# One 512-column matmul for the tokens' high and low halves in the stationary-weight projections

## The chip, the cores and the metric

The kernel runs on one core of a Trainium2 chip. The metric is the device time of one execution in microseconds; the time of the kernel before is the median of three runs.

## What is computed

Two transformer blocks run one after the other on 256 tokens of 2048 channels, in fp32. The first block has two attention layers (one of them with an indexer that selects keys) with a gated output. The second has sparse attention, a gated delta rule and a feed-forward part with 5632 inner channels. Cut to the products that matter here:

```
proj  = rms_norm(x) @ w_in                         # q, k, v, gates; second block: conv inputs, merge gates
o     = attention(q, k, v) * sigmoid-like gate     # the gate is a projection
x     = x + o @ w_out
mixed = g_nsa * (o_nsa @ w_up_nsa) + g_dn * (o_dn @ w_up_dn)
x     = x + mixed @ w_o
x     = x + (silu(h2 @ w_ffn_gate) * (h2 @ w_ffn_up)) @ w_ffn_down
```

## The kernel before, in words

Activations stay in SBUF and every weight is streamed once from DRAM. To keep fp32 accuracy each operand of a product is split into a high and a low part of type fp32r, and a product is three matmuls: high times high, high times low, low times high. The split activations are kept transposed, as pairs of tiles `hi` and `lo` of 128 channels x 4 chunks x 256 tokens (`new_T`, L206 to L209); a full input is four such pairs.

`gemm` (L117 to L160) multiplies the activations with 512 columns of a weight matrix. Its loop over `g` takes 512 rows of the weights at a time: one DMA of 1 MB on SP's queue into `raw` (L134, three buffers), then two tiles of weights, each of two chunks of 128 rows. For each tile ScalarE casts the high part `wh` (L139) and VectorE subtracts the low part `wl` (L140); both have three buffers. After each chunk's matmuls `tick` (L158) advances background work (attention heads, the delta rule), which is written as generators and interleaved with the products in this way. A framework planner then orders each engine's instructions when the program is built.

There are two forms of the product. In the plain one the tokens are stationary and 512 weight columns move (L155 to L157). In the flipped one (`flip=True`) the weights are stationary and 256 tokens move: for each of four blocks of 128 output columns there are three matmuls of 256 columns (L148 to L150), the first with the high tokens, the second with the low tokens, the third with the low weights:

```
o = pt[m // 2][:, (m % 2) * T:(m % 2 + 1) * T]
nc.tensor.matmul(o, wh[:, c, ms], hi[:, kc], start=first and m % 2 == 0, stop=False)
nc.tensor.matmul(o, wh[:, c, ms], lo[:, kc], start=False, stop=False)
nc.tensor.matmul(o, wl[:, c, ms], hi[:, kc], start=False, stop=last and m % 2 == 1)
```

The result of a flipped product is two PSUM banks, each with two blocks of 128 columns x 256 tokens. At the product's end `evac(b, psum)` is called for either bank. PSUM has four such banks (`mm`), taken one at a time.

The flipped form is used for the gate projection of both attention layers (L578, eight products), the inputs of the convolution (L1255, six), the two merge gates (L1276 and L1285, eight), the two up-projections of the mixers (L1278 and L1297, eight products of half the depth), and the feed-forward's gate and up projections (L1329 and L1338, 22). Their evacuations are one VectorE operation that reads PSUM and applies a per-token factor (L573, L1255, L1265, L1327, L1335) or combines it with a gate (L1278, L1290), followed by the nonlinearity and, where the result is the next product's input, by a new split (`split_into`, L521). The feed-forward part takes its inner channels in three blocks of four, four and three column blocks; each block does gate and up projections and then a plain product with `w_ffn_down`.

A helper `slot` (L51) gives temporary tiles out of the buffers of the split activations, alternately from `hi` and `lo` (eight buffers each).

Of the kernel before, what the change touches and what calls it, by code (L numbers as in the profile page):

```python
# [11 lines left out]
F32 = mybir.dt.float32  # L12
F32R = mybir.dt.float32r
# [4 lines left out]
P = 128  # L18
T = 256
# [7 lines left out]
class Kern:  # L27
    """The whole forward pass; activations stay in SBUF, weights stream through once."""

    def __init__(self, ctx, tc, d, out, stop=None):  # L30
# [9 lines left out]
        self.flip = False  # L40
        self.finished = set()

# [32 lines left out]
    def defer(self, n, fn):  # L75
        """trace fn after n further ticks"""
        self.later.append([n, fn])
# [14 lines left out]
    def tick(self):  # L92
        """advance deferred work and the background chains"""
# [27 lines left out]
    def gemm(self, xT, W, c0, n, evac, ng=4, split=False, flip=False):  # L121
# [3 lines left out]
        pt = [self.ps.tile([P, 512], F32, tag="mm", bufs=4, name="mm") for _ in range(2)]  # L125
        for g in range(ng):
# [8 lines left out]
            hi, lo = xT[g]  # L135
            for h in range(2):
                wh = self.sb.tile([P, 2, n], F32R, tag="wh", bufs=3, name="wh")
                wl = self.sb.tile([P, 2, n], F32R, tag="wl", bufs=3, name="wl")
                nc.scalar.copy(wh, raw[:, 2 * h:2 * h + 2])  # L139
                nc.vector.tensor_tensor(wl, raw[:, 2 * h:2 * h + 2], wh.bitcast(F32), ALU.subtract)  # L140
                for c in range(2):
# [9 lines left out]
                    for t in range(0 if flip else 2):  # L151
                        o = pt[t][:, :n]
# [6 lines left out]
        for t in range(2):  # L159
            evac(t, self.c2(pt[t]) if flip else pt[t][:, :n])  # L160
# [18 lines left out]
    def gemm_by_tile(self, xT, W, c0, n, evac, ng):  # L179
        """a narrow gemm that keeps its split weights and ends one token tile before the other"""  # L180
        nc = self.nc
        ws = []
        for g in range(ng):
# [3 lines left out]
            for h in range(2):  # L187
# [4 lines left out]
                ws.append((wh, wl))  # L192
        for t in range(2):
            o = self.ps.tile([P, 512], F32, tag="mm", bufs=4, name="mm")[:, :n]
            ts = slice(t * P, (t + 1) * P)
            for g in range(ng):
                hi, lo = xT[g]
# [8 lines left out]
    def new_T(self):  # L206
        hi = self.sb.tile([P, 4, T], F32R, tag="hi", bufs=8, name="hi")
        lo = self.sb.tile([P, 4, T], F32R, tag="lo", bufs=8, name="lo")
        return hi, lo  # L209

    def to_T(self, src, gain=None, scale=None):
        """src(t, c): [128 tokens, 128 channels]; returns the split transpose of 4 chunks."""
        nc = self.nc
        hi, lo = self.new_T()
# [21 lines left out]
        return hi, lo  # L236
# [7 lines left out]
    def rsq(self, out, in_, mul, n, eps=EPS):  # L244
        """out = (in_ * mul + eps) ** -0.5"""
# [8 lines left out]
    def norm_rstd(self, ss, dst=None):  # L254
        """ss: per token tile [128, 4] block sums of squares -> (rstd, rstd / 2, rstd^2 / 128)"""
# [11 lines left out]
    def rope4(self, o, x, tC, tS, scal=None, heads=4, hd=128):  # L267
        """o = x * C + swap(x) * S over [128, heads, hd]; x in PSUM or SBUF; scal per partition."""
# [20 lines left out]
    def trans4(self, src, dst, scale=None, n=4, eng=None):  # L289
        """dst [128, n*128] = per-128-column-chunk transposes of src [128, n*128]."""  # L290
# [36 lines left out]
    def park_x(self):  # L327
        """the residual waits in DRAM while the mixers need its room"""
# [22 lines left out]
    def gains2(self):  # L351
        """per-channel columns of the second block: conv taps, position embeddings, norm gain"""
# [1156 lines left out]
```

## Time and profile before

| what | value |
|---|---|
| median of 3 runs | 2310.97 us (2310.82 to 2311.34) |
| span of the profiled execution (its own time is not given beside it) | 2308.8 us |
| TensorE matmul, weight load | 2295.5 us, 2094.7 us busy |
| VectorE, ScalarE, GpSimd | 1395.8, 1089.4, 133.6 us busy |
| granted TensorE clock | 0.999 of full |
| moved by DMA | 404.70 MB, mean 175 GB/s |

A page of the profile names engines PE (TensorE matmuls), PEld (TensorE weight loads, which overlap matmuls), DVE (VectorE), ACT (ScalarE), POOL (GpSimd) and SP (SyncE). `L148` is line 148 of the kernel. Rows of grouped instructions have the line, engine, operation, output <- inputs by the program's names, shapes, count, then total busy time in us, mean in ns, and the idle time before them with what ended it. The ends of matmuls are modelled and consecutive records overlap, so the sum of their durations is longer than the time they take.

### The profile page before, as it was taken

Reading aid. Unit: us, or ns where it says so; the run is one execution under the profiler, and the core shown is the slowest. Engines: PE = TensorE matmul, PEld = TensorE weight load, DVE = VectorE, ACT = ScalarE, POOL = GpSimd, SP = SyncE. Lnnn points to the kernel's source line nnn. Section 1 sums busy time; section 2 is a strip of 40 time slices with the busy share of each in tenths; the row PEclk is TensorE's granted clock in tenths of the full one; section 3 lists DMA queues with packets and bytes.
Section 4 is the critical chain, followed back from the end, with each engine's and each line's share of the span. In section 5 each row is a group of like instructions: output and inputs, shape, how many; then the busy total and the mean of one; then the engine's idle time right before and its main releaser. Section 6 shows DMA issues by size and latency. Waiting matters only on the chain.

```text
span 2308.8 us, 39431 instructions
## 1 busy us (share of the span) xinstructions
PE 2295.5 (99%) x16446; PEld 2094.7 (91%) x16446; DVE 1395.8 (60%) x2073; ACT 1089.4 (47%) x1758; POOL 133.6 (6%) x233
## 2 busy tenths in 40 slices
PE   9999999999999999999999999999999999999998
PEld 8878998888998888999999999889998899989997
DVE  5686765656665656878675655555555455554555
ACT  5555644456544434564534444454443344433444
POOL 1011100112100300011101000000000000000000
PEclk9999999999999999999999999999999999999999
DMA  7544455654556754344443665555555555555554
GB/s 230 193 149 153 140 183 182 189 176 137 167 183 208 240 157 152 112 164 130 146 148 120 205 225 183 182 192 191 183 183 189 192 184 183 183 182 184 182 185 143
DMA packets 209811, 404.70 MB, mean 175 GB/s; under 512 B 7376, under 2 KB 25776, under 8 KB 209632
## 3 DMA queue, kind: packets, MB, share of 16 engines
q1 hardware_dynamic: 206880, 394.04, 52.5%
q0 software_dynamic: 2752, 8.13, 1.2%
q8 instruction: 129, 2.11, 0.4%
q14 instruction: 50, 0.41, 0.1%
HBM read 397.95 MB, written 4.19 MB: 174 GB/s over the span
## 4 chain that ended last, share of the span: by engine, by line
PE 99%; DMA 0%; DVE 0%; SPq 0%; ACT 0%; issue 0%; ACTq 0%; POOLq 0%; POOL 0%
PE mm L150 16%; PE mm L148 16%; PE mm L149 16%; PE mm L157 14%; PE mm L156 14%; PE mm L155 14%; PE lg L440 1%; PE tr L294 1%; PE tp L219 1%; PE hid L994 1%; PE nl L1086 0%; PE pt L473 0%; PE ib L638 0%; DMA x<-in_x_dram 0%; PE ov L490 0%; PE ov L491 0%
## 5 line engine op out<-in xcount | busy, mean ns | idle before, releaser
L140 DVE TENSOR_TENSOR wl<-raw,wh 128x1024 fp32r<-128x1024 f32 (+4 forms) x760 | 902.6, 1188 | 794.2 <-ACT wh L139 793.1
L139 ACT CAST wh<-raw 128x1024 fp32r<-128x1024 f32 (+4 forms) x760 | 775.9, 1021 | 1028.5 <-PE mm L149 550.3
L150 PE MATMUL mm<-hi,wl 128*128 128x256 f32 x3072 | 868.9, 284 | 0.0
L148 PE MATMUL mm<-hi,wh 128*128 128x256 f32 x3072 | 868.4, 283 | 0.0
L149 PE MATMUL mm<-lo,wh 128*128 128x256 f32 x3072 | 868.1, 283 | 0.0
L148 PEld LDWEIGHTS mm<-hi,wh 128*128 128x128 f32 x3072 | 579.8, 189 | 1.5 <-issue 0.5
L149 PEld LDWEIGHTS mm<-lo,wh 128*128 128x128 f32 x3072 | 579.2, 189 | 0.8 <-issue 0.2
L150 PEld LDWEIGHTS mm<-hi,wl 128*128 128x128 f32 x3072 | 577.9, 188 | 1.0 <-issue 0.2
L156 PE MATMUL mm<-wl,hi 128*128 128x512 f32 (+4 forms) x1504 | 574.6, 383 | 0.2 <-DVE wl L140 0.2
L157 PE MATMUL mm<-wh,lo 128*128 128x512 f32 (+4 forms) x1504 | 570.6, 381 | 0.0
L155 PE MATMUL mm<-wh,hi 128*128 128x512 f32 (+4 forms) x1504 | 529.3, 382 | 0.0
L156 PEld LDWEIGHTS mm<-wl,hi 128*128 128x128 f32 x1504 | 283.3, 188 | 55.4 <-issue 0.6
L157 PEld LDWEIGHTS mm<-wh,lo 128*128 128x128 f32 x1504 | 283.1, 188 | 55.0 <-issue 1.5
L155 PEld LDWEIGHTS mm<-wh,hi 128*128 128x128 f32 x1504 | 281.1, 189 | 56.2 <-issue 1.3
L248 POOL TENSOR_SCALAR rsqv<-nsum 128x1 f32<-128x1 f32 x10 | 3.5, 351 | 1228.4 <-DVE nsum L1361 744.4
L233 ACT ACTIVATE hi<-tp,gT 128x256 fp32r<-128x256 f32 x64 | 27.6, 471 | 21.3 <-PE tp L219 18.9
L454 ACT ACTIVATE lg<-lg,nb 128x128 f32<-128x128 f32 (+1 forms) x64 | 28.4, 445 | 16.7 <-POOL nb L447 16.7
L234 DVE SCALAR_TENSOR_TENSOR lo<-tp,gT,hi 128x256 fp32r<-128x256 f32 x64 | 28.4, 478 | 12.4 <-ACT hi L233 12.0
L730 DVE SCALAR_TENSOR_TENSOR cv<-raw,cols,cv 128x255 f32<-128x255 f32 (+2 forms) x72 | 31.1, 475 | 1.8 <-ACT cv L727 1.7
L252 ACT ACTIVATE junk<-x 128x512 bf16<-128x512 f32 (+1 forms) x42 | 25.6, 610 | 6.0 <-DMA x<-in_x_dram 2.2
L252 ACT ACTIVATE junk<-mm 128x128 bf16<-128x128 f32 x80 | 22.2, 278 | 7.3 <-PE mm L157 5.8
L440 PE MATMUL lg<-kT,qT 128*128 128x256 f32 (+1 forms) x128 | 23.7, 327 | 0.0
(378 smaller groups left out, 1386.2 us busy)
## 6 DMA issues: line engine op xcount, KB each, us to landing
raw<-in_w_in_dram SPq DMA_DIRECT2D x76, 1024.0 KB, 5.1
raw<-in_w_ffn_gate_dram SPq DMA_DIRECT2D x44, 1024.0 KB, 5.2
raw<-in_w_ffn_up_dram SPq DMA_DIRECT2D x44, 1024.0 KB, 5.2
raw<-in_w_ffn_down_dram SPq DMA_DIRECT2D x41, 1024.0 KB, 5.1
raw<-in_a_w_in_dram SPq DMA_DIRECT2D x40, 1024.0 KB, 5.1
raw<-in_b_w_in_dram SPq DMA_DIRECT2D x40, 1024.0 KB, 5.1
raw<-in_a_w_out_dram SPq DMA_DIRECT2D x16, 1024.0 KB, 5.0
raw<-in_b_w_out_dram SPq DMA_DIRECT2D x16, 1024.0 KB, 5.1
```

What stands on the lines that cost most here:

```text
L139: nc.scalar.copy(wh, raw[:, 2 * h:2 * h + 2])
L140: nc.vector.tensor_tensor(wl, raw[:, 2 * h:2 * h + 2], wh.bitcast(F32), ALU.subtract)
L148: nc.tensor.matmul(o, wh[:, c, ms], hi[:, kc], start=first and m % 2 == 0, stop=False)
L149: nc.tensor.matmul(o, wh[:, c, ms], lo[:, kc], start=False, stop=False)
L150: nc.tensor.matmul(o, wl[:, c, ms], hi[:, kc], start=False, stop=last and m % 2 == 1)
L155: nc.tensor.matmul(o, xh, wh[:, c], start=first, stop=False)
L156: nc.tensor.matmul(o, xh, wl[:, c], start=False, stop=False)
L157: nc.tensor.matmul(o, xl, wh[:, c], start=False, stop=last)
L234: nc.vector.scalar_tensor_tensor(lo[:, k], tp[:, c], g, hi[:, k].bitcast(F32), ALU.mult, ALU.subtract)
L252: self.nc.scalar.activation(self.junk()[:, :w], in_, AF.Square, accum_out=accum)
L440: nc.tensor.matmul(lb[:, i * S:(i + 1) * S], qT[:, h * P:(h + 1) * P], kT[:, :S], start=True, stop=True)
L730: v.scalar_tensor_tensor(o[:, s:], x[:, :T - s], self.convw[:, k:k + 1], o[:, s:], ALU.mult, ALU.add)
```

## The change

The high and low parts of the split activations lie in one tile `hl` of 128 x 4 chunks x 2 x 256, so that a chunk's high and low tokens are 512 adjacent columns. Flipped products become a function of their own, `gemm_T`. It does 256 output columns at a time (`b`), with two blocks of 128 columns, one PSUM bank each. A block takes one matmul of 512 columns (high weights; the results of the high and the low tokens land in two halves of the bank) and one of 256 columns (low weights on high tokens, added to the first half). The bank's halves are added at the evacuation (`joined`): ScalarE copies the second half, VectorE adds the first. A load is 1 MB as before, now 8 chunks of 256 columns. PSUM banks are taken in pairs. The plain product is left as it is but for the pair of banks, and so is the narrow product at the end.

```diff
+    def banks(self):
+        return self.ps.tile([P, 2, 512], F32, tag="mm", bufs=2, name="mm")
+
+    def weights(self, raw, h, n):
+        nc = self.nc
+        k = raw.shape[1] // 2
+        wh = self.sb.tile([P, k, n], F32R, tag="wh", bufs=3, name="wh")
+        wl = self.sb.tile([P, k, n], F32R, tag="wl", bufs=3, name="wl")
+        nc.scalar.copy(wh, raw[:, k * h:k * h + k])
+        nc.vector.tensor_tensor(wl, raw[:, k * h:k * h + k], wh.bitcast(F32), ALU.subtract)
+        return wh, wl
...
-                    for m in range(4 if flip else 0):
-                        o = pt[m // 2][:, (m % 2) * T:(m % 2 + 1) * T]
-                        ms = slice(m * P, (m + 1) * P)
-                        nc.tensor.matmul(o, wh[:, c, ms], hi[:, kc], start=first and m % 2 == 0, stop=False)
-                        nc.tensor.matmul(o, wh[:, c, ms], lo[:, kc], start=False, stop=False)
-                        nc.tensor.matmul(o, wl[:, c, ms], hi[:, kc], start=False, stop=last and m % 2 == 1)
...
+    def gemm_T(self, xT, W, c0, evac, ng=4):
+        nc = self.nc
+        for b in range(2):
+            pt = self.banks()
+            for g2 in range(ng // 2):
+                self.flush(lambda: len(xT) > 2 * g2 + 1 and None not in xT[2 * g2:2 * g2 + 2])
+                raw = self.sb.tile([P, 8, T], F32, tag="raw", bufs=3, name="raw")
+                nc.sync.dma_start(raw, W[g2 * 1024:(g2 + 1) * 1024,
+                                         c0 + b * T:c0 + (b + 1) * T].rearrange("(c p) n -> p c n", p=P))
+                for h in range(2):
+                    wh, wl = self.weights(raw, h, T)
+                    hl = xT[2 * g2 + h][2]
+                    for c in range(4):
+                        first = g2 == 0 and h == 0 and c == 0
+                        last = g2 == ng // 2 - 1 and h == 1 and c == 3
+                        for m in range(2):
+                            ms = slice(m * P, (m + 1) * P)
+                            nc.tensor.matmul(self.c2(pt[:, m]), wh[:, c, ms], hl[:, c],
+                                             start=first, stop=False)
+                            nc.tensor.matmul(pt[:, m, :T], wl[:, c, ms], hl[:, c, 0],
+                                             start=False, stop=last)
+                        if c % 2:
+                            self.tick()
+            p4 = pt.rearrange("p m (s n) -> p m s n", s=2)
+            evac(b, p4[:, :, 0], p4[:, :, 1])
...
+    def joined(self, o, p, q, row=None):
+        self.nc.scalar.copy(o, q)
+        self.nc.vector.tensor_tensor(o, p, o, ALU.add)
+        if row is not None:
+            self.nc.vector.tensor_tensor(o, o, row, ALU.mult)
...
     def new_T(self):
-        hi = self.sb.tile([P, 4, T], F32R, tag="hi", bufs=8, name="hi")
-        lo = self.sb.tile([P, 4, T], F32R, tag="lo", bufs=8, name="lo")
-        return hi, lo
+        hl = self.sb.tile([P, 4, 2, T], F32R, tag="hl", bufs=8, name="hl")
+        return hl[:, :, 0], hl[:, :, 1], hl
...
     def slot(self, name, dt=F32):
-        self.flip = not self.flip
-        return self.sb.tile([P, 2, 512], dt, tag="hi" if self.flip else "lo", bufs=8, name=name)
+        if self.half is not None:
+            b, self.half = self.half, None
+        else:
+            t = self.sb.tile([P, 2, 2, 512], F32, tag="hl", bufs=8, name="half")
+            b, self.half = t[:, 0], t[:, 1]
+        return b if dt is F32 else b.bitcast(dt)
```

Each evacuation of a flipped product takes the two halves and calls `joined` in the place of its first VectorE operation; the up-projections of the mixers join into a tile of their own before they are combined. In the feed-forward part, for example:

```diff
-                def evac_g(b, ps):
-                    v.tensor_tensor(s[b], ps, row, ALU.mult)
+                def evac_g(b, p, q):
+                    self.joined(s[b], p, q, row)
                     nc.scalar.activation(s[b], s[b], AF.Silu)
-                self.gemm(h2, d["w_ffn_gate_2"][0], 512 * jb, 512, evac_g, flip=True)
+                self.gemm_T(h2, d["w_ffn_gate_2"][0], 512 * jb, evac_g)
```

## Rows read from the trace of the kernel before

**Rows 1.** The page: busy time of each engine, and the chain that ended last.
```profile
PE 2295.5 (99%) x16446; PEld 2094.7 (91%) x16446; DVE 1395.8 (60%) x2073; ACT 1089.4 (47%) x1758; POOL 133.6 (6%) x233
...
PE 99%; DMA 0%; DVE 0%; SPq 0%; ACT 0%; issue 0%; ACTq 0%; POOLq 0%; POOL 0%
```

**Rows 2.** TensorE's waits, all execution: us in total, times, longest us.
```profile
PE warm L311 <- DVE zero L308: 1.7, 1, 1.7
...
PE mm L156 <- DVE wl L140: 0.2, 1, 0.2
```

**Rows 3.** Groups of TensorE instructions, shapes apart: busy us, mean ns, idle us.
```profile
L150 PE MATMUL mm<-hi,wl 128*128 128x256 f32 x3072 | 868.9, 284 | 0.0
L148 PE MATMUL mm<-hi,wh 128*128 128x256 f32 x3072 | 868.4, 283 | 0.0
```

**Rows 4.** Timeline of ScalarE, feed-forward part: start us, us, instruction [idle before].
```profile
1651.31 1.05 ACT L139 CAST wh<-raw 128x1024 fp32r<-128x1024 f32 x1 [1.80 <-PE mm L149]
...
1662.70 1.05 ACT L139 CAST wh<-raw 128x1024 fp32r<-128x1024 f32 x1 [1.79 <-PE mm L149]
...
1742.31 1.05 ACT L139 CAST wh<-raw 128x1024 fp32r<-128x1024 f32 x1 [1.73 <-PE mm L157]
...
1759.05 1.05 ACT L139 CAST wh<-raw 128x1024 fp32r<-128x1024 f32 x1 [1.74 <-PE mm L157]
...
1854.82 1.05 ACT L139 CAST wh<-raw 128x1024 fp32r<-128x1024 f32 x1 [1.83 <-PE mm L149]
...
1866.34 1.05 ACT L139 CAST wh<-raw 128x1024 fp32r<-128x1024 f32 x1 [1.83 <-PE mm L149]
...
2013.10 1.05 ACT L139 CAST wh<-raw 128x1024 fp32r<-128x1024 f32 x1 [1.70 <-PE mm L157]
...
2029.90 1.05 ACT L139 CAST wh<-raw 128x1024 fp32r<-128x1024 f32 x1 [1.75 <-PE mm L157]
```

**Rows 5.** Timeline of TensorE where 512 columns give way to 256.
```profile
2282.30 0.39 PE L157 MATMUL mm<-wh,lo 128*128 128x512 f32 x1
2282.53 0.40 PE L155 MATMUL mm<-wh,hi 128*128 128x256 f32 x2
2282.76 0.28 PE L156 MATMUL mm<-wl,hi 128*128 128x256 f32 x1
```

**Rows 6.** Groups of ScalarE and VectorE instructions that read 512 elements from PSUM.
```profile
L298 ACT COPY qT<-tr 128x512 f32<-128x512 f32 x20 | 11.6, 584 | 8.9 <-PE tr L294 8.6
...
L1327 DVE TENSOR_TENSOR sg<-mm,row 128x512 f32<-128x512 f32 x22 | 15.2, 691 | 0.3
```

**Rows 7.** Windows: PE, PEld, DVE, ACT, POOL busy us; PEclk; DMA share; GB/s.
```profile
1025.00:1050.00 25.00, 25.00 (x217) 25.00 (x216) 22.99 (x37) 13.76 (x22) 2.71 (x4) 1.00 0.51 166
...
1571.00:1594.00 23.00, 23.00 (x196) 23.00 (x195) 11.35 (x12) 10.72 (x11) 0.00 (x0) 1.00 0.55 184
1775.00:1797.00 22.00, 22.00 (x97) 17.83 (x96) 10.69 (x11) 8.39 (x8) 0.00 (x0) 1.00 0.57 191
```

**Rows 8.** Timeline of VectorE at the end of an up-projection.
```profile
1593.76 1.40 DVE L1335 TENSOR_TENSOR up<-mm,row 128x512 f32<-128x512 f32 x2
...
1596.28 1.22 DVE L140 TENSOR_TENSOR wl<-raw,wh 128x1024 fp32r<-128x1024 f32 x1
```

**Rows 9.** DMA of 1571 to 1640 us, then of 2271 to 2288 us.
```profile
q1 hardware_dynamic: 6336, 12.58, 55.9%
...
raw<-in_w_ffn_gate_dram SPq DMA_DIRECT2D x8, 1024.0 KB, 5.2
...
q1 hardware_dynamic: 1779, 1.77, 32.4%
...
raw<-in_w_ffn_down_dram SPq DMA_DIRECT2D x5, 512.0 KB, 3.4
```

**Rows 10.** Timeline at the start of the feed-forward part, TensorE and VectorE.
```profile
1547.37 0.28 PE L148 MATMUL mm<-hi,wh 128*128 128x256 f32 x1
...
1556.99 0.48 DVE L234 SCALAR_TENSOR_TENSOR lo<-tp,gT,hi 128x256 fp32r<-128x256 f32 x1
```

More of the change, by code (lines that the diff above doesn't have):

```diff
@@ L39, in __init__ @@
         self.later = []
-        self.flip = False
+        self.half = None
         self.finished = set()
@@ L118, in ready, with gemm @@
             yield
-    def gemm(self, xT, W, c0, n, evac, ng=4, split=False, flip=False):
+    def banks(self):
+        return self.ps.tile([P, 2, 512], F32, tag="mm", bufs=2, name="mm")
+    def weights(self, raw, h, n):
         nc = self.nc
-        pt = [self.ps.tile([P, 512], F32, tag="mm", bufs=4, name="mm") for _ in range(2)]
+        k = raw.shape[1] // 2
[4 more added lines that the diff above has]
+        return wh, wl
+    def gemm(self, xT, W, c0, n, evac, ng=4, split=False):
+        nc = self.nc
+        pt = self.banks()
         for g in range(ng):
@@ L134, in gemm @@
                 nc.sync.dma_start(raw, src)
-            hi, lo = xT[g]
+            hi, lo, _ = xT[g]
             for h in range(2):
[L137 to L140, printed above, removed]
+                wh, wl = self.weights(raw, h, n)
                 for c in range(2):
@@ L144, in gemm @@
                     last = g == ng - 1 and kc == 3
-                    for m in range(4 if flip else 0):
-                        o = pt[m // 2][:, (m % 2) * T:(m % 2 + 1) * T]
-                        ms = slice(m * P, (m + 1) * P)
-                        nc.tensor.matmul(o, wh[:, c, ms], hi[:, kc], start=first and m % 2 == 0, stop=False)
-                        nc.tensor.matmul(o, wh[:, c, ms], lo[:, kc], start=False, stop=False)
-                        nc.tensor.matmul(o, wl[:, c, ms], hi[:, kc], start=False, stop=last and m % 2 == 1)
-                    for t in range(0 if flip else 2):
-                        o = pt[t][:, :n]
+                    for t in range(2):
+                        o = pt[:, t, :n]
                         xh = hi[:, kc, t * P:(t + 1) * P]
@@ L159, in gemm @@
         for t in range(2):
-            evac(t, self.c2(pt[t]) if flip else pt[t][:, :n])
+            evac(t, pt[:, t, :n])
+    def gemm_T(self, xT, W, c0, evac, ng=4):
+        nc = self.nc
+        for b in range(2):
+            pt = self.banks()
+            for g2 in range(ng // 2):
[19 more added lines that the diff above has]
+            evac(b, p4[:, :, 0], p4[:, :, 1])
     @staticmethod
@@ L192, in gemm_by_tile @@
                 ws.append((wh, wl))
+        pt = self.banks()
         for t in range(2):
-            o = self.ps.tile([P, 512], F32, tag="mm", bufs=4, name="mm")[:, :n]
+            o = pt[:, t, :n]
             ts = slice(t * P, (t + 1) * P)
             for g in range(ng):
-                hi, lo = xT[g]
+                hi, lo, _ = xT[g]
                 for c in range(4):
@@ L572, in evac @@
                 gt, th = self.c2(self.w2("gt")), self.c2(self.w2("gth"))
-                nc.vector.tensor_tensor(gt, ps, row, ALU.mult)
+                self.joined(gt, p, q, row)
                 nc.scalar.activation(th, gt, AF.Tanh)
@@ L1148, in values @@
                 b = o[t].rearrange("p (h q) -> p h q", h=4)
-                hi, lo = (x[:, :, t * P:(t + 1) * P] for x in dst)
+                hi, lo = (x[:, :, t * P:(t + 1) * P] for x in dst[:2])
                 nc.scalar.copy(hi, b)
@@ L1253, in second @@
                 raw = [self.c2(self.ev(f"raw{b}")) for b in range(2)]
-                self.gemm(hT, W, 2584 + 1024 * i + 512 * g, 512,
-                          lambda b, ps: v.tensor_tensor(raw[b], ps, row, ALU.mult), flip=True)
+                self.gemm_T(hT, W, 2584 + 1024 * i + 512 * g,
+                            lambda b, p, q: self.joined(raw[b], p, q, row))
                 self.start((kind, g), self.dn_conv(kind, g, raw, st[g]), "de"[g])
@@ L1262, in second, with mgate @@
         md = []
-        def mgate(m, ps):
-            v.tensor_tensor(m, ps, rowh, ALU.mult)
+        def mgate(m, p, q):
+            self.joined(m, p, q, rowh)
             nc.scalar.activation(m, m, AF.Tanh)
```

42 lines of the change are left out of this document (23 added, 19 removed).

## The prediction

> **What bounds the kernel now.** I read the shares and the chain of waits first. TensorE is busy for 2295.5 of 2308.8 us, and the chain that ended last is TensorE for 99% of its length [rows 1]. The waits of TensorE say the same: there are four in the whole execution, the longest 1.7 us and the shortest 0.2 us [rows 2]. So time can only be won by taking time out of TensorE's stream, and only be lost by putting a wait into it.
>
> A busy TensorE is not yet a rate, because records overlap: the 256-column matmuls are shown with 284 ns each [rows 3], though 9216 of them at that length would be longer than the span. The true spacing comes from ScalarE's weight casts. Each cast waits for TensorE to release a tile, so cast after cast shows how long one tile of weights keeps TensorE. A tile is 24 matmuls of 256 columns in the stationary-weight products, and 12 of 512 columns in the others.
>
> - Stationary weights, first block of the feed-forward part: four intervals between 1651.31 and 1662.70, 2.848 us each [rows 4], so **118.7 ns** per matmul.
> - The same in the second block: four intervals between 1854.82 and 1866.34, 2.880 us each [rows 4], so **120.0 ns**. I see no reason in the rows for this 1%.
> - 512 columns: six intervals between 1742.31 and 1759.05, 2.790 us each [rows 4], so **232.5 ns**.
>
> Two matmuls of 256 columns thus cost 237.4 ns, one of 512 costs 232.5. What the change can win on TensorE is this difference, some 5 ns each time two become one.
>
> **What is removed on TensorE.** Today one block of 128x128 weights takes three matmuls of 256 columns: high weights on high tokens, high weights on low tokens, low weights on high tokens. Each line has 3072 [rows 3], and that is 48 products of 64 blocks. Afterwards a block takes one matmul of 512 and one of 256 columns, so 3072 matmuls and as many weight loads go.
>
> - Old tile: 2.848 us. New tile, 8 of each width: 8 x 232.5 + 8 x 118.7 = 2.809 us. Saved 0.039 us.
> - 14 of the 48 products (gate and up of the feed-forward's second and third blocks, seven column blocks) run at the slower pace: there 512 columns are at 2.800 us a tile too, six intervals between 2013.10 and 2029.90 [rows 4], or 233.3 ns. 2.880 us against 8 x 233.3 + 8 x 120.0 = 2.827 us. Saved 0.053 us.
> - 48 products have 8 tiles each. (34 x 8) x 0.039 + (14 x 8) x 0.053 = 10.6 + 5.9 = **16.5 us**.
>
> The new operand shape does not stand in the trace: widths that alternate matmul by matmul. The nearest row is where the stream changes from 512 to 256 columns: the last 512 keeps its 0.23 us and the first two of 256 take 0.23 us together [rows 5], so that step adds nothing. The step from 256 back to 512 is not shown. I bound the pair from both sides. Below: the small matmul at half the price of the large, 116.3 ns, which would save 25 us instead of 16.5. Above: no gain at all, the joint matmul at the price of two. I take the sum of the two measured spacings, since both widths, with a fresh weight load ahead of each matmul, are what those rows timed.
>
> The Trainium skill ("TensorE: Matmul & The Clock Gate", section "Back-to-back issue gap") gives an isolated gap of N/2.4 + 2.5 ns, so a dropped matmul would be worth 2.5 ns and the change, as an estimate, 3072 x 2.5 = 7.7 us. The trace does not agree with that page: its 118.7 and 232.5 ns are well above the page's 109.2 and 215.8, and my sum goes by the trace.
>
> **What is added beside it.** The evacuation of a half product has one ScalarE copy out of PSUM and one VectorE addition more. There are 52 products (eight have half the depth), so 104 halves. At 0.58 us for a copy of 512 elements and 0.69 us for a VectorE operation of the same size [rows 6], that is 60 us of ScalarE and 72 us of VectorE. Per half (about 11.2 us) 0.6 and 0.7 us go into engines which in the feed-forward stage are busy 10.7 and 11.35 of 23 us [rows 7]. I cost it at nothing: weight tiles are triple-buffered, so when a half ends two later tiles are ready and cover about 5.6 us.
>
> How that cover is used today can be seen at an up-projection's end. VectorE begins to evacuate at 1593.76 and the next low-half subtraction runs at 1596.28, 1.22 us long [rows 8]: it is done 3.7 us after the product ended, with 1.9 us to spare. Afterwards VectorE handles 512 elements instead of 1024 at a time, but waits for ScalarE's copy first: 0.58 + 3 x 0.69 + 1.22 = 3.9 us, or 4.9 us if a 1.05 us cast [rows 4] is placed ahead of the copy. Still within 5.6 us, but by 0.7 to 1.7 us. This is the thinnest part of my argument.
>
> **Edits that cost nothing, and why.**
>
> - Loads: four of 1 MB per full product before and after, on the same SP queue, but in runs of 1 KB instead of 2 KB. 6336 packets took 55.9% of 16 engines for 69 us, 97 ns each; where the kernel loads 256 columns, 1779 packets took 32.4% of 17 us, 50 ns each [rows 9]. Twice the packets at half the time: the share stays near 56%. Landing was 5.2 us for 1 MB and 3.4 us for half of it in 1 KB runs [rows 9]; three buffers of 5.6 us each stand between a load and its use, which covers another microsecond.
> - Token tiles: high and low parts lie in one buffer, with as many bytes in all. The buffers of the first operand are now read until the second half, so they come free later; the mixed result's third block waits for that, but is read only a product and a half later.
> - PSUM: banks are handed out in pairs; a pair comes back once copy and addition are done, some 2 us after its half, and is next wanted one half (5.6 us or more) later.
> - Background steps: 16 ticks per full product as before, so attention and delta-rule work stay at the same density.
> - Start of the feed-forward part: the fourth token block is wanted at three quarters of a half instead of a whole product. The first matmul is at 1547.37 and the block's last low part ends at 1556.99 + 0.48 [rows 10]. Three quarters of a half (8.4 us of 11.24) after the first matmul is 1555.8; the four chunks are wanted 0.7 us apart from there on, the last at 1557.9, and VectorE makes them in turn. No stall, or a few tenths.
>
> **Sum.** 2308.8 - 16.5 = 2292.3 us of span. The median of the runs, 2310.97, is 2.2 us above the profiled span (the profile gives no own time beside it); I keep that: **2294.5 us**.
>
> **Rivals.**
>
> 1. *The weight loads were the limit, and are relieved.* In the 256-column stage weight loads cover all 23.00 of 23 us, in the 512-column stage 17.83 of 22 [rows 7]. If it is the load and not the columns that sets 118.7 ns, the 512-column matmul lets the next load finish early and the small matmul falls to 116.3 ns: 25 us gained, **2286 us**. Against it: the loads are longer than their own spacing, so a full row is only overlap. Beside this: the Trainium skill ("Perfetto Trace Analysis", section "Identifying the Most-Contended Engine") takes weight-load busy share as the better measure of TensorE's headroom; by it this stage is full and the rival stands. Chance 0.10.
> 2. *Columns alone count.* The stream still moves 768 columns per block. If the joint matmul costs nearly what its two parts did, the gain is at most half of mine, 0 to 8 us: **2303 to 2311 us**. The 232.5 ns speaks against the zero end. Chance 0.13. The 7.7 us that follow from the Trainium skill's page on TensorE lie at this rival's better end.
> 3. *The low half of the weights comes late after each half product.* The place: the first weight tile that VectorE makes after a half, behind an addition which itself waits for ScalarE's copy. It decides when that tile is ready over 5.6 us after the half's end, which takes 0.7 to 1.7 us more than I worked out: another cast and the split of the result ahead of it, or the stage of the delta rule, where VectorE is already busy 22.99 of 25 us [rows 7]. At 0.4 us in each of 104 halves it costs 42 us: **2336 us**; at 0.16 us it eats the gain. Today's single wait of this kind, 0.2 us [rows 2], speaks against it. Chance 0.14.
> 4. *The change does not do what it says*: if the joint operand or its output were not one run, TensorE's pace would not change, **2311 us**. By the diff both are contiguous. Chance 0.03.
>
> **How the numbers follow.** The forecast has 0.60, at 2289 to 2303 us. Faster by over 0.2% (4.6 us, about what a measurement of this kernel can tell from no change) means below 2306.4: the forecast, rival 1 and 0.05 of rival 2, together 0.75. Within 0.2%: the rest of rival 2 and rival 4, 0.11. Slower: rival 3, 0.14. The range reaches into rival 1 below and the mildest part of rival 3 above: 2283 to 2313 us.
>
> **What would show it.** Right: casts in the feed-forward's gate and up stage 2.81 us apart; 3072 matmuls of 512 columns and 3072 of 256 where there were 9216; TensorE still 99% busy; DMA share near 56%; no wait of TensorE on VectorE's low halves. Rival 1 shows as casts 2.79 us apart, rival 2 as 2.83 to 2.85. Rival 3 shows as waits of TensorE or its loads on the subtraction, in regular places 11 us apart. I would be wrong altogether if TensorE's share fell below 98%.

## The result, and the profile after

The changed kernel is slower: 2349.82 us (median of 4 runs, 2346.89 to 2349.86) against 2311.15 (4 runs of before beside it), a ratio of 1.0164 with a 95% interval of 1.0152 to 1.0176. The profiled execution took 2346.89 us with a span of 2345.1.

The page of the changed kernel, in the order of [rows 1, 3, 9]: busy time, the granted clock in 40 slices, the main DMA queue, the chain that ended last, and the two new groups of matmuls.

```profile
PE 2294.7 (98%) x13374; PEld 1954.5 (83%) x13374; DVE 1465.4 (62%) x2177; ACT 1139.2 (49%) x1862; POOL 138.8 (6%) x233
...
PEclk9999999999999999999979999999999999999999
...
q1 hardware_dynamic: 305184, 394.04, 52.5%
...
PE 96%; DVE 2%; ACT 1%; DMA 0%; issue 0%; POOL 0%; SPq 0%; ACTq 0%; POOLq 0%; DVEq 0%
...
L189 PE MATMUL mm<-hl,wh 128*128 128x512 f32 x3072 | 1086.6, 395 | 4.7 <-DVE un L205 3.2
L191 PE MATMUL mm<-hl,wl 128*128 128x256 f32 x3072 | 873.2, 284 | 0.0
```

The matmuls are what the diff promised, and 3072 instructions and loads are gone. But TensorE's busy time is what it was, one slice in the middle has a lower clock, and the chain is no longer TensorE alone. Its waits, which came to four small ones before [rows 2], are now (us in total, times, longest):

```profile
PE cvb L785 <- DVE cv L780: 10.3, 3, 3.7
PE mm L163 <- DVE un L205: 4.4, 1, 4.4
PE tr L338 <- DVE qkn L815: 4.3, 2, 3.7
PE mm L189 <- DVE un L205: 3.2, 1, 3.2
PE ov L533 <- ACT half L521: 2.7, 2, 1.7
...
PE ib L682 <- ACT rel L684: 2.0, 3, 1.5
```

Most are small background work (convolution, delta rule, attention) waiting for its own last step. That is no cause yet: it shows that nothing else was there to fill the gaps. To find where, I cut the execution at the first load of each weight on SP's queue; the stages that changed are in this table, with the runs told of below (us; ratio to before with its interval). "Inputs" runs from the second block's first input weights to its first nsa up-projection, "joins" from there to its first delta-rule up-projection, "FFN" from its first gate load to the first load of its last, narrow product. The stages are read from the profiled execution, the times are medians.

| kernel | layer A, to its output weights | inputs | joins | FFN | time, ratio |
|---|---|---|---|---|---|
| before | 309.3 | 373.5 | 200.4 | 751.8 | 2311.15 |
| **after** | **319.2** | **366.9** | **246.6** | **741.0** | **2349.82, 1.0164** |
| e1 pairs only | 314.8 | 382.7 | 200.0 | 751.9 | 2326.02, 1.0063 (1.0048 to 1.0078) |
| e2 single banks | 311.5 | 361.2 | 245.4 | 740.5 | 2330.46, 1.0083 (1.0068 to 1.0098) |
| e3 own buffer | 318.8 | 368.5 | 220.2 | 741.0 | 2320.50, 1.0042 (1.0027 to 1.0057) |
| e4 both | 311.6 | 361.3 | 216.2 | 740.5 | 2301.48, 0.9960 (0.9946 to 0.9974) |
| e5 halves only | 310.0 | 373.6 | 200.4 | 751.8 | 2311.09, 1.0000 (0.9991 to 1.0009) |
| e6 temporaries only | 310.3 | 373.6 | 205.0 | 751.8 | 2315.96, 1.0022 (1.0013 to 1.0032) |
| e7 FFN alone | 309.7 | 373.5 | 200.4 | 740.5 | 2299.01, 0.9947 (0.9931 to 0.9964) |
| e8 both, z later | 312.1 | 361.2 | 210.5 | 740.5 | 2295.98, 0.9935 (0.9920 to 0.9950) |
| e9 one pair held | 317.2 | 368.1 | 236.1 | 741.0 | 2339.66, 1.0119 (1.0105 to 1.0133) |
| e10 old gates in A | 310.3 | 361.3 | 210.5 | 740.5 | 2293.30, 0.9922 (0.9909 to 0.9936) |
| e11 FFN and up | 310.1 | 373.5 | 219.3 | 740.5 | 2318.14, 1.0028 (1.0017 to 1.0040) |
| e12 FFN and z | 309.7 | 373.5 | 200.6 | 740.5 | 2299.23, 0.9948 (0.9935 to 0.9962) |

So the FFN gained 10.8 us; layer A lost 9.9 and the joins 46.2. (The inputs' 6.6 us are no plain gain: background work moved out of them into the joins, see e4.) In both places TensorE stands still and then runs at a lower clock. The windows of the changed kernel, columns as in [rows 7]:

```profile
125.00:150.00 25.00, 23.01 (x98) 16.36 (x98) 19.79 (x50) 13.08 (x32) 1.62 (x3) 0.88 0.40 127
...
1150.00:1175.00 25.00, 18.18 (x118) 15.89 (x117) 15.14 (x24) 13.12 (x35) 2.42 (x4) 0.93 0.37 115
1175.00:1200.00 25.00, 13.80 (x72) 12.49 (x72) 18.79 (x38) 9.92 (x28) 2.89 (x6) 0.59 0.00 1
...
1250.00:1275.00 25.00, 19.96 (x99) 16.82 (x99) 8.14 (x10) 8.87 (x25) 2.42 (x4) 0.86 0.14 42
```

In the worst of them no weights arrive at all (DMA share 0.00) and TensorE is busy for 13.80 of 25 us, with a mean clock of 0.59. The timeline around it:

```profile
1166.16 0.28 PE L191 MATMUL mm<-hl,wl 128*128 128x256 f32 x1
...
1193.87 1.07 ACT L204 COPY un<-mm 128x512 f32<-128x512 f32 x2
...
1200.96 1.21 DVE L205 TENSOR_TENSOR un<-mm,un 128x512 f32<-128x512 f32 x2
...
1201.63 0.50 PE L189 MATMUL mm<-hl,wh 128*128 128x512 f32 x1 [3.24 <-DVE un L205]
```

The first nsa up-projection's last matmul starts at 1166.16. Both of its halves ("x2") are copied only at 1193.87 and added at 1200.96, and the next product starts at 1201.63: no large matmul for **35 us**. The target `un` is a new tile from the pool of 28 working tiles, which the delta rule and the convolutions draw on too. Not all of the 35 us is the wait for it: the copies end at 1194.94 and the additions start 6 us later, and in between VectorE works through delta-rule steps that stand ahead of them. The second nsa up-projection stops in the same way: its last matmul starts at 1245.28, the next large one at 1261.04 (the row of 1250 us).

In layer A the rows are different. First the evacuation of the values' product in the kernel before, ScalarE's high and VectorE's low part of token tile 0, then ScalarE's high part of tile 1:

```profile
140.46 0.68 ACT L549 ACTIVATE vh<-mm,st 128x512 fp32r<-128x512 f32 x1
141.17 0.75 DVE L550 SCALAR_TENSOR_TENSOR vl<-mm,st,vh 128x512 fp32r<-128x512 f32 x1
141.29 0.70 ACT L549 ACTIVATE vh<-mm,st 128x512 fp32r<-128x512 f32 x1
```

The same three in the changed kernel:

```profile
141.55 0.68 ACT L593 ACTIVATE vh<-mm,st 128x512 fp32r<-128x512 f32 x1
142.94 0.75 DVE L594 SCALAR_TENSOR_TENSOR vl<-mm,st,vh 128x512 fp32r<-128x512 f32 x1
143.72 0.69 ACT L593 ACTIVATE vh<-mm,st 128x512 fp32r<-128x512 f32 x1 [1.22 <-DVE vl L594]
```

ScalarE's read of token tile 1 now waits for VectorE's read of token tile 0, though they touch different banks and different results. Before, the two overlapped. The two banks are now one tile, and that is all that ties them together. Behind the waiting ScalarE sit the top-k scores, for which TensorE waits in turn (the `ib` row above). This is the row of 125 us; the rest of layer A's loss lies between 225 and 275 us (3.25 us idle, then a clock of 0.93) and is taken up at e8 and e10.

From this came two theories. **Pool:** the sums of the up-projections come late because their tile does, and meanwhile hold the PSUM banks. **Pair:** one tile over two banks puts reads of different engines in an order that nothing needs. The rivals: the added copies themselves, or the buffers now shared by high and low halves.

### The profile page after: what moved, and what is told of

Its sections match the earlier page's. It is cut to its first block, busy times and chain, and to the rows that moved or that the text cites. A ratio compares the mean times of both kernels' runs of the same rounds, so it can differ in the third digit from the quotient of the medians.

```text
span 2345.1 us, 33491 instructions
## 1 busy us (share of the span) xinstructions
PE 2294.7 (98%) x13374; PEld 1954.5 (83%) x13374; DVE 1465.4 (62%) x2177; ACT 1139.2 (49%) x1862; POOL 138.8 (6%) x233
## 3 DMA queue, kind: packets, MB, share of 16 engines
q1 hardware_dynamic: 305184, 394.04, 52.5%
## 4 chain that ended last, share of the span: by engine, by line
PE 96%; DVE 2%; ACT 1%; DMA 0%; issue 0%; POOL 0%; SPq 0%; ACTq 0%; POOLq 0%; DVEq 0%
PE mm L189 30%; PE mm L191 16%; PE mm L163 14%; PE mm L164 14%; PE mm L165 14%; PE lg L484 1%; PE tp L263 1%; PE tr L338 1%; PE hid L1038 1%; PE pt L517 0%; PE nl L1130 0%; DVE cv L774 0%; ACT junk L296 0%; DVE wl L136 0%; PE ib L682 0%
## 5 line engine op out<-in xcount | busy, mean ns | idle before, releaser
L189 PE MATMUL mm<-hl,wh 128*128 128x512 f32 x3072 | 1086.6, 395 | 4.7 <-DVE un L205 3.2
L191 PE MATMUL mm<-hl,wl 128*128 128x256 f32 x3072 | 873.2, 284 | 0.0
L189 PEld LDWEIGHTS mm<-hl,wh 128*128 128x128 f32 x3072 | 577.7, 188 | 136.1 <-DVE un L205 3.4
L163 PE MATMUL mm<-wh,hl 128*128 128x512 f32 (+4 forms) x1504 | 577.1, 384 | 5.2 <-DVE un L205 4.4
L191 PEld LDWEIGHTS mm<-hl,wl 128*128 128x128 f32 x3072 | 578.4, 188 | 1.5 <-issue 0.2
L164 PE MATMUL mm<-wl,hl 128*128 128x512 f32 (+4 forms) x1504 | 576.5, 384 | 0.0
L165 PE MATMUL mm<-wh,hl 128*128 128x512 f32 (+4 forms) x1504 | 574.6, 382 | 0.0
L163 PEld LDWEIGHTS mm<-wh,hl 128*128 128x128 f32 x1504 | 284.8, 189 | 61.7 <-DVE un L205 4.6
L164 PEld LDWEIGHTS mm<-wl,hl 128*128 128x128 f32 x1504 | 284.9, 189 | 56.1 <-issue 1.5
L165 PEld LDWEIGHTS mm<-wh,hl 128*128 128x128 f32 x1504 | 284.7, 189 | 55.7 <-issue 1.3
L277 ACT ACTIVATE hl<-tp,gT 128x256 fp32r<-128x256 f32 x64 | 27.9, 474 | 14.2 <-DVE hl L278 10.5
L278 DVE SCALAR_TENSOR_TENSOR hl<-tp,gT,hl 128x256 fp32r<-128x256 f32 x64 | 28.5, 478 | 4.2 <-ACT hl L277 4.0
```

Source lines behind the costliest of these rows:

```text
L163: nc.tensor.matmul(o, xh, wh[:, c], start=first, stop=False)
L164: nc.tensor.matmul(o, xh, wl[:, c], start=False, stop=False)
L165: nc.tensor.matmul(o, xl, wh[:, c], start=False, stop=last)
L189: nc.tensor.matmul(self.c2(pt[:, m]), wh[:, c, ms], hl[:, c], start=first, stop=False)
L191: nc.tensor.matmul(pt[:, m, :T], wl[:, c, ms], hl[:, c, 0], start=False, stop=last)
L278: nc.vector.scalar_tensor_tensor(lo[:, k], tp[:, c], g, hi[:, k].bitcast(F32), ALU.mult, ALU.subtract)
```

## The experiments

**e1, e2: the pair, put in alone and taken out.** In the kernel before (and likewise in its narrow product at the end):

```diff
-        pt = [self.ps.tile([P, 512], F32, tag="mm", bufs=4, name="mm") for _ in range(2)]
+        pb = self.ps.tile([P, 2, 512], F32, tag="mm", bufs=2, name="mm")
+        pt = [pb[:, 0], pb[:, 1]]
```

> The kernel before with one thing of the change: a product's two PSUM banks are one tile of two banks (two such tiles instead of four single ones); the old products, no temporaries, no shared halves. Pair theory: the ScalarE read of the second token tile is put behind VectorE's read of the first, so layer A loses its 8 to 12 us here too: the first load of the first layer's output weights moves from 311.9 to 318 to 324 us, the time is 2318 to 2325 us, and there is no stop of 20 us in the second block. Rival (the shared halves of the activation tiles, or the extra copies, cost layer A its 10 us): no change, 2309 to 2314 us.

In the changed kernel, the reverse. The join then has to be cut in two as well, so this edit is not the pair alone:

```diff
-        self.nc.scalar.copy(o, q)
-        self.nc.vector.tensor_tensor(o, p, o, ALU.add)
+        for m in range(2):
+            self.nc.scalar.copy(o[:, m], q[m])
+            self.nc.vector.tensor_tensor(o[:, m], p[m], o[:, m], ALU.add)
```

> The changed kernel with single PSUM banks as separate tiles again; the join of the two halves of a bank is then two copies and two additions of 256 columns in place of one of 512. Pair theory: layer A is back, first load of the first layer's output weights at 309 to 313 us instead of 321.8, and the time falls by 8 to 14 us to 2334 to 2342 us; the second block still stops. Rival (extra copies are the cost): there are more of them, so the time is 2350 to 2360 us, layer A included.

Measured 2326.02 and 2330.46 us, the first 1 us above what I expected, the second 3.5 us below (its layer A's first output load, 314.0, 1 us above): the pair costs 15 us put in alone and 19 us taken out, although e2 has more evacuation instructions. For this loss the rival of the bare copies is out. I had the place half right: layer A's first output load comes at 317.4 in e1 (expected 318 to 324), and the second block's inputs lose 9.2 us, which I had not expected. There, too, e1's TensorE waits for work behind evacuations: three waits on VectorE (keys, rope, low values) of 2.5, 1.5 and 0.8 us that the kernel before does not have, and one 25 us stretch at a clock of 0.93. The windows of e1 repeat the changed kernel's row of the same stretch almost to the digit:

```profile
125.00:150.00 25.00, 23.01 (x99) 16.38 (x98) 19.80 (x50) 13.08 (x32) 1.55 (x3) 0.88 0.39 127
150.00:175.00 25.00, 25.00 (x116) 20.46 (x115) 19.71 (x42) 12.00 (x26) 1.81 (x5) 0.98 0.49 151
```

These two rows account for e1's layer A: 1.99 us idle, and 25 x 0.12 + 25 x 0.02 = 3.5 us of clock, together 5.5; the table has 314.8 - 309.3 = 5.5. In e2 the reads overlap again:

```profile
141.22 0.75 DVE L594 SCALAR_TENSOR_TENSOR vl<-mm,st,vh 128x512 fp32r<-128x512 f32 x1
141.34 0.70 ACT L593 ACTIVATE vh<-mm,st 128x512 fp32r<-128x512 f32 x1
```

Beside this: the Trainium skill ("PSUM — Partial Sum Buffer", section "PSUM bank collisions raise a hardware error") forbids two engines in one bank and the same quadrant at once, and allows different banks. The e2 rows agree with the second half: two engines read two banks at the same time. The order in the changed kernel is wider than that rule asks for.

**e3: the sums in a buffer of their own.** The rope table's buffer is free by then:

```diff
-                up = self.c2(self.w2("un"))
+                up = self.c2(self.rb("un"))
```

and the same for `ud`, where `rb` is the single [128, 512] buffer of the rope table.

> The changed kernel; only the temporaries of the up projections (un, ud) leave the pool of 28 working tiles for a buffer of their own (that of the rope table, free by then). Pool theory: the stretch from the first nsa up-projection load to the first delta-rule up-projection load falls from 246.6 us back to 196 to 204 us (200.4 before), no slice with the clock at 0.59, and the time is 2302 to 2312 us; layer A stays 8 to 12 us late. Rival (the copies themselves, queued on ScalarE behind the delta rule, hold the banks): the stretch stays above 230 us and the time above 2335 us.

Measured 2320.50 us: 29.3 us back from one edit of an address. The joins fall from 246.6 to 220.2, and the stretch whose clock was 0.59 (1175 to 1200 us) now has it at 1.00; the 0.59 in this row is the DMA share:

```profile
1175.00:1200.00 25.00, 25.00 (x154) 22.13 (x153) 20.20 (x29) 16.92 (x37) 4.61 (x6) 1.00 0.59 182
```

All eight copies into `un` are still there; the first starts at 1161.39, 1.2 us after its half's last matmul has started. So the rival falls. Which use of the pool the tile waited for, no run shows. And I expected 196 to 204 us and 2302 to 2312 us of time: 20 us of the joins stay.

**e4: both.**

> Single banks and own buffer together. If pool and pair theory are both right and nothing else was lost, the two gains add: before minus the 11 us of the FFN, minus 1 to 3 us for each of the two layers and the gated join: 2290 to 2299 us, faster than both kernels. If one of them is wrong, or the join in smaller pieces costs more than the pairs did, 2305 us or more.

Measured 2301.48 us. The two gains add: 19.4 + 29.3 = 48.7 expected, 48.3 measured. It is faster than before by 0.4%, but 2.5 us short of what I expected at worst. Some of the joins' length is work moved: the inputs take 12.2 us less than before, the joins 15.8 more, and 1044 of the background's matmuls start in the inputs and 964 in the joins, where it was 1221 and 786 in the kernel before. One stop is left, in e4's timeline:

```profile
1280.70 2.00 ACT L1231 ACTIVATE sz<-mm,rstd 128x512 f32<-128x512 f32 x4
...
1285.44 0.77 PE L193 MATMUL mm<-hl,wh 128*128 128x512 f32 x1 [4.28 <-DVE sz L1233]
```

Here the two z products are evacuated together from 1280.70 on. The last matmul of the first one started at 1217.22, so it held two banks for 63 us; the second took the other two, and a gate product waits 4.28 us for them. The targets `sz` come from the same pool, but no run shows whether it is the tile or its place in ScalarE's order that makes this evacuation late; in the kernel before it is 24 us late as well (1227.54 to 1252.07) and stops nothing.

**e5, e6, e7: one part of the change at a time in the old scheme.** e5 takes only the shared buffers, e6 only the temporaries (here that of the delta rule's up-projection; `un` likewise):

```diff
-                v.scalar_tensor_tensor(m[b], m[b], 1.0, ps, ALU.add, ALU.mult)
+                up = self.c2(self.w2("ud"))
+                nc.scalar.copy(up, ps)
+                v.scalar_tensor_tensor(m[b], m[b], 1.0, up, ALU.add, ALU.mult)
```

e7 is e2 with `gemm_T` left in the FFN alone, and the old flipped product everywhere else.

> The kernel before with one thing of the change: the high and low parts of an activation block share one buffer, and the attention's probability tiles take halves of such a buffer. Layer A of the run with both repairs still takes 311.6 us to its output weights where 309.3 less some 2 for the gates was due. If the shared buffers hold the attention up, this kernel's layer A is 2 to 5 us longer than before (311 to 314 us) and the time is 2313 to 2317 us. If the missing 4 us lie in the joins of the gates' halves, it is 2309.5 to 2312.5 us and layer A 309 to 310 us.

> The kernel before with one thing of the change: the up projections' sums are first copied into a tile of the pool of 28 (16 copies of 0.58 us on ScalarE) and multiplied from there; old products, single banks, old buffers. Pool theory: the first product's copies come after the delta rule of the second group has let tiles go, its banks are held and the stretch between the first nsa and the first delta-rule up-projection load grows from 200.4 to 220 to 245 us: 2328 to 2352 us. Rival (the stop needs the pairs, or the products' faster pace, as well): under 2318 us. Copies at their bare cost, hidden: 2311 us.

> New products in the FFN alone, single PSUM banks; gates, convolution inputs and up projections by the old products, so no temporaries; shared halves stay. If the FFN's gain of 11 us stands by itself and the halves cost nothing: 2298 to 2302 us. If the halves cost layer A 2 to 4 us: 2301 to 2305 us. If the new products in the layers and in the second block were worth what the cadence says (about 10 us), the run with both repairs should have beaten this one by as much; it took 2301.5 us, so equality says that they are given back there.

Measured 2311.09, 2315.96 and 2299.01 us. The shared halves cost nothing. The FFN's gain stands by itself. And e6 goes against the simple pool theory: the same temporaries cost 5 us where taking them out of the changed kernel gave 29. Late sums alone are not enough.

**e9, e11: what makes a late sum expensive.** In the old product a late sum of 512 columns holds two of four banks, one for each half, and the other two carry the next whole product. In the new one a half of 256 columns takes two banks, its high and low parts side by side: one late product holds all four. e9 gives the first half the rope buffer and leaves the second half in the pool:

```diff
-                up = self.c2(self.w2("un"))
+                up = self.c2(self.rb("un") if b == 0 else self.w2("un"))
```

e11 puts the new product, with its pool temporaries, into the nsa up-projections of e7.

> The changed kernel; the sum of the first half of each nsa up projection has a buffer of its own, that of the second half still comes from the pool. If the stop is both pairs of banks being held by late sums at once, one late sum holds one pair, the other carries the products on, and the stretch between the first nsa and the first delta-rule up-projection load falls from 246.6 to 220 to 230 us (220.2 with both sums in a buffer of their own): 2320 to 2331 us. If a late tile costs its lateness wherever it sits, at least half of the 26 us stay: 2333 us or more.

> New products in the FFN and in the four nsa up projections, whose sums come from the pool of 28; everything else as in the run with the FFN alone (2299.0 us), single banks. Old products with the same late sums cost 5 us. If a half of the new product, which takes two banks where the old one took one, is what turns late sums into a stop, all four banks are held here and the stretch between the first nsa and the first delta-rule up-projection load grows from 200.4 to 220 to 240 us: 2318 to 2338 us. If the stop needs the faster pace of the products before it, 2302 to 2308 us.

e11: 2318.14 us, joins 200.4 to 219.3, so +18.9 where the old products with late sums had +4.6. The pace of the products ahead is the old one there, so that rival is out. The sums of e6 are even the later ones. In e6 the first nsa up-projection's last matmul starts at 1156.68; the next product starts 0.12 us behind it, and the sums are copied only at 1173.72:

```profile
1156.68 0.28 PE L150 MATMUL mm<-hi,wl 128*128 128x256 f32 x1
1156.80 0.28 PE L148 MATMUL mm<-hi,wh 128*128 128x256 f32 x1
...
1173.72 1.06 ACT L1280 COPY un<-mm 128x512 f32<-128x512 f32 x2
```

In e11 the copies come 9 us after the last matmul and the additions 16 us after it, and until then no large matmul runs:

```profile
1156.26 0.28 PE L191 MATMUL mm<-hl,wl 128*128 128x256 f32 x1
...
1172.27 1.34 DVE L230 TENSOR_TENSOR un<-mm,un 128x256 f32<-128x256 f32 x4
...
1172.68 0.58 PE L215 MATMUL mm<-hl,wh 128*128 128x256 f32 x1 [3.46 <-DVE un L230]
```

In the second nsa up-projection the sums are 39 us late in e6 and 13 in e11. So the lateness alone does not set the price; what differs is how many banks the late product holds. One part is not told apart from this: a new product's banks come back only after VectorE's addition, and between e11's copies and additions (1166.39 to 1172.27) VectorE is busy with delta-rule steps. The windows of the two, first e11:

```profile
1150.00:1175.00 25.00, 17.16 (x109) 15.84 (x109) 23.92 (x49) 9.54 (x18) 0.00 (x0) 0.88 0.24 83
```

and e6:

```profile
1150.00:1175.00 25.00, 25.00 (x217) 25.00 (x216) 23.01 (x37) 12.90 (x18) 0.00 (x0) 1.00 0.50 169
```

e9 went against me: 2339.66 us, joins 236.1, so 15.9 of the 26.4 us stay, and the rival's number came. But e9 did not keep one pair free, as its rows show:

```profile
1243.46 0.39 PE L169 MATMUL mm<-wh,hl 128*128 128x512 f32 x1
...
1270.32 0.58 ACT L208 COPY un<-mm 128x512 f32<-128x512 f32 x1
1270.79 0.70 ACT L1231 ACTIVATE sz<-mm,rstd 128x512 f32<-128x512 f32 x1
...
1273.17 0.73 PE L193 MATMUL mm<-hl,wh 128*128 128x512 f32 x1 [4.41 <-DVE un L209]
```

The second nsa up-projection's last matmul started at 1217.84, and its second half is copied at 1270.32. The other pair carries the first z product on, whose last matmul starts at 1243.46; then that pair is held too, until ScalarE has taken the second half's copy and turns to `sz`. No large matmul runs for 29.7 us. Before that, with one pair held, new halves wait for their own joins (a wait on a gate's join at 1180.26, 2.18 us, another of 2.7, and 5.25 us idle between 1175 and 1200 us). So two banks carry an old product on, and a new one only with waits; what one held pair alone would cost, e9 does not tell.

**e8, e10, e12: towards a faster kernel.** e8 is e4 with the first z product moved from the third gated join to the fourth:

```diff
-            if j == 2:
+            if j == 3:
                 self.gemm(hT, W, 5656, 512, lambda t, ps: z_part(t, ps, 0))
-            if j == 3:
                 self.gemm(hT, W, 6168, 264, lambda t, ps: z_part(t, ps, 512))
```

e10 is e8 with the old products for layer A's gates. e12 is e7 with z moved.

> Both repairs, and the product of the delta rule's gate z (512 columns) moved one gated join later, to just ahead of its second part. In the run with both repairs TensorE waits 4.3 us at 1281 us for that product's evacuation, whose target tiles come late from the pool while two of the four banks are held, and its clock falls to 0.86 in that stretch. If the late target is the cause, holding the banks for a shorter time gives back 4 to 8 us: 2293 to 2298 us. If the wait only moves, 2300 to 2304 us.

> Both repairs and the later z product, with layer A's four gate products by the old scheme (all 512 columns, then both halves evacuated). New gate products end their first half half a product earlier and then ask for the attention's result; in layer A, whose attention starts late, that exposes its chain: TensorE idles 2.5 us between 225 and 275 us. If so, layer A's time to the output weights falls from 312.1 to 309 to 310.5 us and the whole to 2293 to 2295 us. If the loss is the shared buffers' or the banks', it stays at 2295 to 2297 us.

> New products in the FFN alone, with the z product one gated join later. If z's place matters only where the new products hold two banks for a half, this is the run with the FFN alone again, 2297.5 to 2300.5 us, and the new products in the second block are worth 3 us. If moving z helps the old products as well, 2292 to 2296 us, and the new products bring nothing outside the FFN.

Measured 2295.98, 2293.30 and 2299.23 us, all as the theory had it. In e8 the first z product holds its banks for 25 us after its last matmul (1258.98 to 1284.32) instead of 63, and the stop is gone. z's place gives 5.5 us with the new products and nothing with the old ones, which fits the banks held. In layer A the windows of e8, then of e10:

```profile
225.00:250.00 25.00, 23.50 (x145) 20.49 (x145) 16.83 (x39) 14.23 (x47) 4.71 (x9) 1.00 0.36 114
250.00:275.00 25.00, 23.95 (x146) 20.92 (x146) 20.34 (x43) 17.22 (x40) 1.04 (x3) 1.00 0.42 128
```

```profile
225.00:250.00 25.00, 25.00 (x206) 24.63 (x205) 19.55 (x42) 17.96 (x51) 6.01 (x9) 1.00 0.42 133
250.00:275.00 25.00, 25.00 (x205) 24.64 (x205) 19.67 (x40) 15.40 (x35) 0.66 (x3) 1.00 0.42 136
```

The 2.55 us that TensorE idles in e8 are gone. In e8 1.3 us of them are a wait of the attention for its own probabilities and 0.8 a wait for a gate's join; neither wait is in e10. That a first half which ends earlier asks for the attention's result too early fits this, but e10 swaps the whole gate product, so the early question and the join are not told apart. **e10 is faster than both kernels**, by 0.78% and 2.4%.

## Why the prediction was wrong

I forecast 2294.5 us, range 2283 to 2313; 2349.82 came out.

**The gain on TensorE was right.** Casts in the changed kernel's FFN, first in its first block and then in its second, to be held against [rows 4]:

```profile
1690.74 1.05 ACT L135 CAST wh<-raw 128x1024 fp32r<-128x1024 f32 x1 [1.77 <-PE mm L189]
...
1710.40 1.05 ACT L135 CAST wh<-raw 128x1024 fp32r<-128x1024 f32 x1 [1.27 <-PE mm L189]
...
1867.02 1.05 ACT L135 CAST wh<-raw 128x1024 fp32r<-128x1024 f32 x1 [1.63 <-PE mm L189]
...
1878.26 1.05 ACT L135 CAST wh<-raw 128x1024 fp32r<-128x1024 f32 x1 [1.27 <-PE mm L189]
```

Seven intervals of 2.809 us and four of 2.810. I had said 2.81 for the first block and 2.827 for the other two, where the old products ran 1% slower; that 1% is gone (the third block's 24 intervals from 2144.43 us on are 2.809 us on average). The FFN should have gained 8 x 8 x 0.039 + 14 x 8 x 0.053 = 8.4 us; it gained 10.8, and 11.3 with single banks. Over the whole kernel e10 gains 18.1 us (2311.36 beside it) where the sum said 16.5, though four of its 48 products are the old ones and one other product is moved. That the total comes so close is partly luck: the FFN gives 11.3 us instead of 8.4, everything else 6.8 instead of 8.1. The 7.7 us by the Trainium skill's page on TensorE ("TensorE: Matmul & The Clock Gate", section "Back-to-back issue gap"), as an estimate, are beaten by the FFN alone. Rival 1 wanted intervals of 2.79 us, rival 2 of 2.83 to 2.85; neither came.

**Evacuations: "I cost it at nothing".** The reason I gave, that three weight tiles cover them, held. In the products, TensorE's weight loads waited for the low halves of weights twice, 0.4 us in all:

```profile
PEld mm L164 <- DVE wl L136: 0.4, 2, 0.2
```

So rival 3, at the right end of the scale (2336 us), had the wrong place. Under this head I asked only who needs VectorE after a half, and not what the copy itself has to wait for.

**The step that failed is "PSUM: … a pair comes back once copy and addition are done, some 2 us after its half".** At the first nsa up-projection it came back 35 us after the last matmul, at the second 16. Three things stand behind this, none of them in my text:

- The sum needs a tile, and in the two up-projections that tile is new. I counted the copy's 0.58 us and not the buffer that it writes: it comes from a pool that background work is using at this moment. A buffer of its own gives 29.3 us (e3). This overlaps with the next point.
- A half now holds two banks where it held one. What four banks cover is half of what it was. Old products whose first two sums come 17 and 39 us late lose 5 us (e6), new ones with 16 and 13 us lose 19 (e11).
- I took the pairs as a matter of handing out banks. One tile also ties together the reads of its two token tiles, in the 512-column products, which the change does not even touch. 15 us put in alone (e1), 19 us taken out together with the cut of the join (e2).

**Other edits that I had at nothing.** The shared halves cost nothing (e5); the loads' share is 52.5% for the whole execution, as it was before, and 58.2% from 1600 to 1690 us in the FFN, where I had said 56%; and no wait appears at the start of the FFN. That "attention and delta-rule work stay at the same density" was true in ticks, but the new gate products of layer A cost 2.7 us (e10), perhaps because its attention is asked for half a product earlier.

**What would show it.** "I would be wrong altogether if TensorE's share fell below 98%" was a poor gauge. The share is 97.85% (2294.7 of 2345.1 us, printed as 98%), a hair beyond the sign, in a kernel that is 1.6% slower: TensorE's records at the lower clock are longer, so it is busy as long as before with 3072 instructions fewer. The waits named the place, the stage table the size.

With these places repaired the time lies where the forecast had it: 2349.8 less 48.3 (e4), 5.5 (e8) and 2.7 (e10) is 2293.3 us. That is another kernel than the one I forecast, with one product moved and four left as they were.

## What to carry to other kernels

When an evacuation gets a temporary, ask which pool it comes from and who else holds that pool at that moment; the temporary's lateness is paid in PSUM banks, and the price grows when each output takes more of them. Don't join banks into one tile unless their readers belong together. To find such a loss, cut the execution at the first load of each weight: it showed gains and losses by stage at once, where the shares of the whole showed nothing.

## What the runs showed that I had not expected

A wait can cost more than its length. After TensorE's gaps at 142 to 146 us in the changed kernel, the next large matmuls start 0.43 us apart instead of 0.23:

```profile
147.18 0.63 PE L165 MATMUL mm<-wh,hl 128*128 128x512 f32 x1
147.60 0.63 PE L163 MATMUL mm<-wh,hl 128*128 128x512 f32 x1
148.03 0.63 PE L164 MATMUL mm<-wl,hl 128*128 128x512 f32 x1
```

The granted clock from 147 to 149 us, columns as in [rows 7], is 0.50, the 1.2 GHz level:

```profile
147.00:149.00 2.00, 2.00 (x6) 1.52 (x6) 1.75 (x4) 1.04 (x6) 0.72 (x2) 0.50 0.03 8
```

With 1.99 us idle, this stretch lost another 3 to 3.5 us to the clock. The 1.50 and 1.05 us of idle time in e8's two rows of layer A cost no clock: it stays at 1.00 there. The idle time of a stretch alone does not tell which it will be: the changed kernel's 3.35 us between 850 and 875 us leave the clock at 1.00, and e1's 3.34 us in the same stretch go with 0.93.

Three things stay open. First, what makes the tiles of the pool and the first z product's evacuation come so late was not followed to its source. Second, the timed runs of the changed kernel lie at 2349.8 us and its profiled one at 2346.9; e9 shows the same (2339.5 to 2340.0, profiled 2335.6), and no run tells why. Third, why the old products ran 1% slower in the second and third FFN blocks, and the new ones do not, was not tried.
